# Encoder layer on one core: adaLN dots put at other places, one block sum dropped, loads and stores issued by three engines, and a fixed order in the gate stage

## The chip, the cores and the metric

The kernel runs on one core of a Trainium2 chip. The metric is the device time of one execution in microseconds; runs are compared by their median. The times before are 1262.81, 1264.8 and 1268.21 us.

Five engines run at once, each through its own instructions in its own order: TensorE (PE, matmuls), VectorE (DVE), ScalarE (ACT), GpSimd (POOL) and SyncE (SP). DMAs are issued by an engine, here by SP, POOL or ACT, and an issue waits in that engine's order until what it needs is free.

## The reference

One layer, 1024 positions, width 1024, all in float32:

```python
mod = jax.nn.silu(c) @ w_ada + b_ada
sh1, sc1, gt1, sh2, sc2, gt2 = jnp.split(mod[:, None, :], N_MOD, axis=-1)

h = rmsnorm(x, norm1_g) * (1.0 + sc1) + sh1
z = h @ w_in
...
a_out = gmlp_branch(u, v, gm_v_g, gm_w_s, gm_b_s) @ w_a
b_out = window_attention_branch(q, k, va, q_norm_g, k_norm_g, attn_sink) @ w_b
merged = jax.nn.sigmoid(gate_a) * a_out + jax.nn.sigmoid(gate_b) * b_out
x = x + gt1 * (merged @ w_o)

h2 = rmsnorm(x, norm2_g) * (1.0 + sc2) + sh2
f_gate, f_up = jnp.split(h2 @ w_ffn_in, 2, axis=-1)
x = x + gt2 * ((jax.nn.silu(f_gate) * f_up) @ w_ffn_out)
```

u, v, q, k, va and the two gates are column blocks of z. w_ada has 6 x 1024 columns; the kernel works in units of 128 of them (a *column* below), with 1024 numbers for each of 128 partitions.

## The kernel before, in words

**Products.** Every float32 product is made of three matmuls on a high and a low part of each operand (`mm3`). A weight unit of 128 x 1024 is loaded into a tile `raw` (three buffers, SP, L137), ACT copies its high part to `wh`, and DVE subtracts to get the low part `wl` (`unit`). PE waits for both.

**Stages**, in us of the profile: half 0 of the positions (q and k, v, attention, projections), 0 to 212; the q/k loop of half 1, 212 to 252; its v, u and attention, 252 to 350; its projection loop over d = 0 to 7, which here also prepares the gates (the *joint stage*), 358 to 404; the gates, 404 to 524; the output projection w_o, half 0 to 575 and half 1 to 627; then the FFN to the end.

**adaLN dots.** The first 16 columns are worked off at the start. 32 more stand in `ada_queue`, and the code takes them from it where it has a place: `ada_load` loads one column of 512 KB into a `raw` tile, `ada_next` lets DVE make the dot with silu(c) (one 128 x 1024 operation, and a small one for the result) and loads the next. `ada_half_load` loads a column as two halves into the two `hs` stream buffers, and `ada_half` makes two operations of 128 x 512 and two small ones. The places: six full dots in the d loop of half 0, five in the q/k loop of half 1 (k = 2, 3, 5, 6, 7), ten columns in the gate stage (five full, five in halves), eleven full ones in the output projection of half 0.

**Joint stage.** The gates of all d are computed by a scheme of Strassen's kind: seven products instead of eight (`GSTEP`, twelve matmuls each), on sums of blocks of the normalised x and on sums of blocks of the weights w_ga and w_gb. `block_sums(k, part, kinds)` makes the sums of x for a chunk k of four; it reads four chunk tiles a0, a1 (`hs`, two buffers) and b0, b1 (`xs`, two buffers), loaded from DRAM (x0d, x1sd) by `block_load`. Each sum has a high part (ACT) and a low part (DVE, `block_part`). The two parts of a chunk stand behind the projections d = 2k and 2k + 1. A projection's result for d > 1 is stored to `pd` (256 KB, POOL, L140).

**Gate stage.** For each d from 2 to 7 seven steps; step 6 of a d comes behind step 0 of the next. `gate_load(d + 1)` (two 512 KB loads of SP) comes behind step 3, `gate_prep_a`, `_b` and `_c` turn them into four weight units. `branch_load` brings 1 MB of `pd` back, `gating` combines it with the gates and stores to `md`; the output projection loads md through `m_load`.

**Order.** In each engine a scheduler places instructions by estimated readiness, except where `in_order[0]` is set: there they stay in the order of the code. Loads through `load` always stay in the code's order on SP. Rows of half 1 in the gate loop, the d loop and the o loop are those below.

## Time and profile before

| what | value |
|---|---|
| runs | 1262.81, 1264.8, 1268.21 us; median 1264.8 us |
| profiled execution, and its span | 1266.84 us, 1265.0 us |
| PE busy | 1227.7 us, 97% of the span, 5634 matmuls |
| DVE busy | 911.8 us, 72% |
| ACT busy | 574.0 us, 45% |
| POOL busy | 161.5 us, 13% |
| moved by DMA | 236.28 MB, mean 187 GB/s |

A busy PE can still be a slow one, since a matmul is counted as busy whatever clock was granted; that clock stands beside the busy times by stage. The chain of waits tells, for each stretch, what ended last. In rows of the time line, the bracket holds the engine's idle time ahead of a row and what ended it. Nearly all compute rows have line L76, that of the helper which records them; they are told apart by the names of their tiles.

### The profile page before, as it was taken

Reading aid. Unit: us, or ns where it says so; the run is one execution under the profiler, and the core shown is the slowest. Engines: PE = TensorE matmul, PEld = TensorE weight load, DVE = VectorE, ACT = ScalarE, POOL = GpSimd, SP = SyncE. Lnnn points to the kernel's source line nnn. Section 1 sums busy time; section 2 is a strip of 40 time slices with the busy share of each in tenths; the row PEclk is TensorE's granted clock in tenths of the full one; section 3 lists DMA queues with packets and bytes.
Section 4 is the critical chain, followed back from the end, with each engine's and each line's share of the span. In section 5 each row is a group of like instructions: output and inputs, shape, how many; then the busy total and the mean of one; then the engine's idle time right before and its main releaser. Section 6 shows DMA issues by size and latency. Waiting matters only on the chain.

```text
span 1265.0 us, 15583 instructions
## 1 busy us (share of the span) xinstructions
PE 1227.7 (97%) x5634; PEld 1012.8 (80%) x5634; DVE 911.8 (72%) x1496; ACT 574.0 (45%) x930; POOL 161.5 (13%) x202
## 2 busy tenths in 40 slices
PE   6999999899998999999999999999999999999998
PEld 4888887788886877767888888888888887888887
DVE  9898885387887787876798766677666676455646
ACT  5567854167866332434555233333332334433342
POOL 1223332023321000001100000000110000010001
PEclk9999999999999999999999999999999999999999
DMA  9632178422147445597721453554645549886652
GB/s 368 242 100 91 44 236 313 150 84 67 51 147 256 171 175 206 201 315 269 249 108 59 174 195 125 179 200 182 217 166 176 191 167 333 290 325 188 195 165 100
DMA packets 76272, 236.28 MB, mean 187 GB/s; under 512 B 9122, under 2 KB 9122, under 8 KB 70179
## 3 DMA queue, kind: packets, MB, share of 16 engines
q1 hardware_dynamic: 60626, 163.45, 38.2%
q0 software_dynamic: 15568, 71.84, 15.1%
q8 instruction: 44, 0.72, 0.2%
q14 instruction: 34, 0.27, 0.1%
HBM read 178.11 MB, written 57.15 MB: 186 GB/s over the span
## 4 chain that ended last, share of the span: by engine, by line
PE 63%; issue 12%; DMA 10%; DVE 9%; ACT 4%; POOL 0%; SPq 0%; ACTq 0%; DVEq 0%; POOLq 0%
PE mm L76 32%; PE at L76 31%; DVE mid L76 3%; DVE wl L76 2%; DMA raw<-in_w_gb_dram 2%; DMA raw<-in_w_o_dram 2%; DMA raw<-in_w_ada_dram 2%; ACT wh L76 1%; ACT mid L76 1%; DMA raw<-in_w_ab_dram 1%; DVE raw L76 1%; DMA mid<-in_w_ada_dram 1%; DMA wo<-in_w_out_dram 1%; ACT lb L76 1%; DMA wS<-wo 1%
## 5 line engine op out<-in xcount | busy, mean ns | idle before, releaser
L76 ACT CAST wh<-raw 128x1024 fp32r<-128x1024 f32 x155 | 162.6, 1052 | 183.9 <-PE mm L76 57.4
L76 DVE TENSOR_TENSOR wl<-raw,wh 128x1024 fp32r<-128x1024 f32 x141 | 172.2, 1222 | 96.3 <-ACT wh L76 92.4
L76 PE MATMUL mm<-mid,wh 128*128 128x512 f32 x704 | 218.9, 392 | 7.1 <-ACT wh L76 3.1
L76 PEld LDWEIGHTS mm<-mid,wh 128*128 128x128 f32 x704 | 131.7, 188 | 37.4 <-ACT wh L76 5.2
L76 PE MATMUL at<-j,wh 128*128 128x512 f32 x464 | 142.8, 389 | 0.0
L76 PE MATMUL mm<-mid,wl 128*128 128x512 f32 x352 | 138.5, 393 | 4.0 <-DVE wl L76 3.9
L76 PE MATMUL mm<-wh,h 128*128 128x512 f32 x384 | 129.9, 400 | 2.3 <-ACT h L76 2.1
L76 PEld LDWEIGHTS at<-j,wh 128*128 128x128 f32 x464 | 87.0, 188 | 18.2 <-ACT xs L76 0.2
L76 DVE TENSOR_TENSOR wl<-ws,wh 128x1024 fp32r<-128x1024 f32 (+1 forms) x55 | 62.0, 1128 | 43.7 <-ACT wh L76 43.7
L76 PE MATMUL mm<-j,wh 128*128 128x512 f32 x288 | 90.6, 396 | 0.0
L76 PE MATMUL at<-j,wl 128*128 128x512 f32 x232 | 90.3, 389 | 0.0
L76 PE MATMUL at<-h,wh 128*128 128x512 f32 x288 | 89.1, 391 | 0.7 <-DVE mid L76 0.7
L76 PEld LDWEIGHTS mm<-wh,h 128*128 128x128 f32 x384 | 72.0, 190 | 17.2 <-ACT h L76 3.0
L76 PE MATMUL mm<-h,wh 128*128 128x512 f32 x272 | 84.6, 392 | 0.0
L76 PEld LDWEIGHTS mm<-mid,wl 128*128 128x128 f32 x352 | 66.2, 188 | 21.8 <-DVE wl L76 8.3
L76 ACT CAST wh<-ws 128x1024 fp32r<-128x1024 f32 (+1 forms) x55 | 53.6, 974 | 59.0 <-DVE ws L76 42.5
L76 PE MATMUL mm<-wl,h 128*128 128x512 f32 x192 | 76.3, 397 | 0.1
L76 PEld LDWEIGHTS mm<-j,wh 128*128 128x128 f32 x288 | 55.1, 192 | 11.6
L76 PEld LDWEIGHTS at<-h,wh 128*128 128x128 f32 x288 | 53.8, 188 | 12.5 <-DVE mid L76 1.5
L76 DVE TENSOR_TENSOR ol<-raw,oh 128x1024 fp32r<-128x1024 f32 x30 | 36.7, 1224 | 31.7 <-ACT oh L76 31.5
L76 PEld LDWEIGHTS mm<-h,wh 128*128 128x128 f32 x272 | 50.6, 188 | 10.3
L76 ACT ACTIVATE xs<-xs 128x512 f32<-128x512 f32 x21 | 13.3, 633 | 97.2 <-DVE xs L76 97.2
(273 smaller groups left out, 2545.0 us busy)
## 6 DMA issues: line engine op xcount, KB each, us to landing
raw<-in_w_gate_dram SPq DMA_DIRECT2D x28, 512.0 KB, 5.1
raw<-in_w_ada_dram SPq DMA_DIRECT2D x27, 512.0 KB, 5.4
tA<-hid POOLq DMA_DIRECT2D x11, 1024.0 KB, 5.0
tB<-hid POOLq DMA_DIRECT2D x11, 1024.0 KB, 5.0
wo<-in_w_out_dram POOLq DMA_DIRECT2D x22, 512.0 KB, 6.3
wS<-wo POOLq DMA_DIRECT2D x11, 1024.0 KB, 5.2
raw<-wS SPq DMA_DIRECT2D x44, 256.0 KB, 3.8
raw<-tB SPq DMA_DIRECT2D x44, 256.0 KB, 4.3
```

The costliest lines, as they stand in the source:

```text
L76: ins = f(*args, **kw)
```

## The change: what it does

* **Dots.** The 32 columns are placed anew: five (not six) in the d loop of half 0; four in halves in the q/k loop of half 1, through `hs` and `xs` in turn, loaded at k = 2 and 3 and dotted at k = 4 to 7; five in halves in the attention steps 1 to 5 of half 1 (none before); twelve in halves in the gate stage (one in d = 2, three in d = 3, 4, 5 each, two in d = 6); four through `ada_pair_load`, two columns in one 1 MB load of POOL into a big buffer, in the output projection of half 0; two in halves at d = 0 and 1 of half 1.
* **One block sum less.** N2 is gone: step 3 uses T2 = b1 + a0, B22 is negated in place by ACT, and signs of the evictions change. A chunk has four sums and six low parts on DVE instead of five and six, in another order: b0 and a0 come free first.
* **Issuing engines.** Chunk loads, branch loads and md loads are issued by POOL instead of SP, the pd stores by ACT instead of POOL. SP keeps weights, x and halves of w_ada columns.
* **Gate stage.** It stays in the order of the code. `gate_load(d + 1)` comes right behind the steps 0 and 6 that open a d (in d = 2 behind step 1) instead of behind step 3. The projection of branch a for d = 7 is held back and runs behind step 1 of d = 2.
* The row statistics and modulations in the output projection of half 1 come somewhat later.

```diff
-    def ada_half_load():
+    def ada_half_load(tag="hs"):
...
+    def ada_pair_load():
+        i = ada_queue[0][0] - GT1
+        t = midt(F32, 2)
+        store(t, w_ada2[i : i + 2].rearrange("a p b -> p a b"))
...
-            load(chunk[name], (x0d if name[0] == "a" else x1sd)[4 * int(name[1]) + k])
+            store(chunk[name], (x0d if name[0] == "a" else x1sd)[4 * int(name[1]) + k])
...
             V.tensor_tensor(b1, b1, b0, op=ALU.subtract)
...
+            low3 = block_part("T3", k, b1, kinds[1], dsh[:, c])
+            V.tensor_tensor(b0, b0, a0, op=ALU.subtract)
+            low1 = block_part("T1", k, b0, kinds[1])
+            low3()
+            added(b1, a0)
+            low2 = t2()
...
+            block_load(k + 1, "b0")
+            for x in blk["B22"]:
+                A.activation(x[:, k, :], x[:, k, :].bitcast(F32), AF.Copy, scale=-1.0)
             return
...
+        low, low1 = b11(), b21()
+        low()
         low1()
-        block_load(k + 1, "b0")
+        block_load(k + 1, "a0")
+        V.tensor_tensor(a1, b1, a1, op=ALU.subtract)
+        low = block_part("T4", k, a1, kinds[2])
+        block_load(k + 1, "b1")
         low()
...
+        block_load(k + 1, "a1")
...
-    GSTEP = ((0, 0, "B11", 0), (1, 0, "T3", 1), (0, 1, "B21", 0), (2, 0, "N2", 2),
+    GSTEP = ((0, 0, "B11", 0), (1, 0, "T3", 1), (0, 1, "B21", 0), (2, 0, "T2", 2),
...
-        load(flat(branch_t[d]), pd[d])
+        store(flat(branch_t[d]), pd[d])
...
-            if hf == 1 and k == 1:
-                ada_load()
-            elif hf == 1 and k and k != 4:
-                ada_next(k < 7)
+            if hf == 1 and k in (2, 3):
+                ada_half_load(("hs", "xs")[k % 2])
+            elif hf == 1 and k > 3:
+                ada_half(("hs", "xs")[k % 2] if k < 6 else None)
...
+            if hf == 1 and 0 < s < 6:
+                ada_half("hs" if s < 5 else None)
...
-            for x in ("a1", "b0", "b1", "a0"):
+            for x in ("b0", "a0", "b1", "a1"):
...
+                if hf and d == KT - 1 and br == 0:
+                    held.append((wab[d], t))
+                    continue
...
-                    store(pd[d][:, j * Q : (j + 1) * Q], c)
+                    nc.scalar.dma_start(pd[d][:, j * Q : (j + 1) * Q], c)
...
-        load(t, md[hf][k])
+        store(t, md[hf][k])
...
+        if d == 2:
+            gate_step(d, 0)
+            gate_evict(d, 0)
+            gate_step(d, 1)
+            held_projection()
+            low_c = gate_prep_c(d)
+            gate_evict(d, 1)
+            low_c()
+            gate_load(d + 1)
...
         gate_step(d, 0)
         gate_evict(d, 0)
...
+        gate_step(d - 1, 6)
+        low_c = gate_prep_c(d)
+        gate_evict(d - 1, 6)
+        low_c()
+        if not last:
+            gate_load(d + 1)
...
-            gate_load(d + 1)
...
         if not last:
+            low_b()
+            if d in (3, 4, 5):
+                ada_half("hs")
+            low_s()
+            ada_half("hs" if d < KT - 2 else None)
...
-                ada_next()
-                if 2 < d < 6:
-                    ada_next()
+                if d in (0, 2):
+                    ada_pair_load()
+                if 0 < d < 5:
+                    ada_next(False)
+                if d == 7:
+                    ada_half_load()
```

What that does to the engines' orders is seen at three places. First DVE in the q/k loop of half 1. Before, a full dot (the rows with `silu_c`) stands between two low parts `wl` of the q and k weights:

```order
L76 TENSOR_TENSOR wl_2215<-raw_2212,wh_2214 128x1024
L76 SCALAR_TENSOR_TENSOR raw_2316,acc_mod<-raw_2316,silu_c 128x1024
L76 TENSOR_TENSOR wl_2258<-raw_2255,wh_2257 128x1024
L76 TENSOR_SCALAR mod<-acc_mod,cc 128x1
L76 SCALAR_TENSOR_TENSOR raw_2341,acc_mod<-raw_2341,silu_c 128x1024
L76 TENSOR_SCALAR mod<-acc_mod,cc 128x1
L76 TENSOR_TENSOR wl_2292<-raw_2289,wh_2291 128x1024
L76 SCALAR_TENSOR_TENSOR raw_2374,acc_mod<-raw_2374,silu_c 128x1024
L76 SCALAR_TENSOR_TENSOR mod<-acc_mod,badap,cc 128x1
```

After, the same stretch, from the low part that opens it; dots are halves from `hs` and `xs`:

```order
L76 TENSOR_TENSOR wl_2169<-raw_2128,wh_2168 128x1024
L76 SCALAR_TENSOR_TENSOR hs_2333,acc_mod<-hs_2333,silu_c 128x512
L76 TENSOR_TENSOR wl_2211<-raw_2208,wh_2210 128x1024
L76 SCALAR_TENSOR_TENSOR hs_2334,part_2395<-hs_2334,silu_c 128x512
L76 TENSOR_TENSOR acc_mod<-acc_mod,part_2395 128x1
L76 TENSOR_SCALAR mod<-acc_mod,cc 128x1
L76 TENSOR_TENSOR wl_2254<-raw_2251,wh_2253 128x1024
L76 SCALAR_TENSOR_TENSOR xs_2366,acc_mod<-xs_2366,silu_c 128x512
L76 TENSOR_TENSOR wl_2288<-raw_2285,wh_2287 128x1024
L76 SCALAR_TENSOR_TENSOR xs_2367,part_2431<-xs_2367,silu_c 128x512
```

The dots have moved some low parts further back, and none of them reads a `raw` tile any more.

Second, the loads of the joint stage. Before, SP issues chunk loads (`x0d`, `x1sd`) and the projection weights `w_ab` in one order:

```order
L137 DMA hs_3852<-x0d 128x512
L137 DMA raw_3858<-in_w_ab_dram 128x1024
L137 DMA hs_3903<-x0d 128x512
L137 DMA raw_3909<-in_w_ab_dram 128x1024
L137 DMA xs_3948<-x1sd 128x512
L137 DMA xs_3951<-x1sd 128x512
L137 DMA hs_3953<-x0d 128x512
L137 DMA raw_3959<-in_w_ab_dram 128x1024
L137 DMA hs_4004<-x0d 128x512
L137 DMA raw_4010<-in_w_ga_dram 128x1024
L137 DMA raw_4012<-in_w_gb_dram 128x1024
```

After, SP has the weights alone:

```order
L137 DMA raw_3860<-in_w_ab_dram 128x1024
L137 DMA raw_3915<-in_w_ab_dram 128x1024
L137 DMA raw_3966<-in_w_ab_dram 128x1024
L137 DMA raw_4017<-in_w_ab_dram 128x1024
L137 DMA raw_4068<-in_w_ga_dram 128x1024
L137 DMA raw_4070<-in_w_gb_dram 128x1024
L137 DMA hs_4204<-in_w_ada_dram 128x512
L137 DMA hs_4205<-in_w_ada_dram 128x512
```

and POOL has the chunk loads, with the stores to `md` of the first two d among them:

```order
L140 DMA hs_3900<-x0d 128x512
L140 DMA xs_3852<-x1sd 128x512
L140 DMA md_108<-t_778_3747 128x512
L140 DMA xs_3906<-x1sd 128x512
L140 DMA md_108<-t_780_3751 128x512
L140 DMA hs_3909<-x0d 128x512
L140 DMA hs_4004<-x0d 128x512
L140 DMA xs_3958<-x1sd 128x512
L140 DMA xs_4008<-x1sd 128x512
L140 DMA hs_4011<-x0d 128x512
L140 DMA hs_4108<-x0d 128x512
```

The chunk loads have left SP's order; in POOL's they stand one behind another and behind stores.

Third, DVE from the last steps of d = 3 in the gates to the first of d = 4. Before, a full dot from `raw` and one in halves stand among the evictions (`mid`) and the sums of weight blocks (rows of `raw` and `wl`):

```order
L76 TENSOR_TENSOR raw_4371<-raw_4371 128x512
L76 SCALAR_TENSOR_TENSOR raw_4416,acc_mod<-raw_4416,silu_c 128x1024
L76 SCALAR_TENSOR_TENSOR hs_4423,acc_mod<-hs_4423,silu_c 128x512
L76 TENSOR_TENSOR mid_4298<-at_4357,xs_4296 128x512
L76 TENSOR_TENSOR wl_4458<-raw_4371,wh_4457 128x1024
L76 SCALAR_TENSOR_TENSOR mid_4298<-mid_4298,mid_4213 128x2048
L76 TENSOR_TENSOR mid_4442<-mm_4467,xs_4440 128x512
L76 TENSOR_TENSOR mid_4298<-mid_4298 128x512 x2
L76 SCALAR_TENSOR_TENSOR mod<-acc_mod,badap,cc 128x1
L76 SCALAR_TENSOR_TENSOR hs_4424,part_4562<-hs_4424,silu_c 128x512
L76 TENSOR_TENSOR acc_mod<-acc_mod,part_4562 128x1
L76 SCALAR_TENSOR_TENSOR mod<-acc_mod,badap,cc 128x1
```

After, two columns in halves follow each other with three operations between, ahead of the next eviction and the low part of the last weight unit:

```order
L76 TENSOR_TENSOR wl_4464<-raw_4383,wh_4463 128x1024
L76 SCALAR_TENSOR_TENSOR hs_4424,acc_mod<-hs_4424,silu_c 128x512
L76 SCALAR_TENSOR_TENSOR hs_4425,part_4484<-hs_4425,silu_c 128x512
L76 TENSOR_TENSOR acc_mod<-acc_mod,part_4484 128x1
L76 TENSOR_SCALAR mod<-acc_mod,cc 128x1
L76 TENSOR_TENSOR raw_4381<-raw_4381,t_910_4460 128x512
L76 TENSOR_TENSOR raw_4381<-raw_4381 128x512
L76 TENSOR_TENSOR t_914_4467<-t_910_4460,t_913_4466 128x512
L76 SCALAR_TENSOR_TENSOR hs_4489,acc_mod<-hs_4489,silu_c 128x512
L76 SCALAR_TENSOR_TENSOR hs_4490,part_4496<-hs_4490,silu_c 128x512
L76 TENSOR_TENSOR acc_mod<-acc_mod,part_4496 128x1
L76 TENSOR_SCALAR mod<-acc_mod,cc 128x1
```

Both columns use the two `hs` buffers, so the load of the second stands behind the first one's operations.

More of the change, by code (lines that the diff above doesn't have):

```diff
@@ L531, in ada_half_load, with ada_half @@
             ada_halves.append((col, gain, t))
-    def ada_half(more=True):
+    def ada_pair_load():
+        i = ada_queue[0][0] - GT1
+        t = midt(F32, 2)
+        store(t, w_ada2[i : i + 2].rearrange("a p b -> p a b"))
+        for j in range(2):
+            col, gain = ada_queue.pop(0)
+            ada_ahead.append((col, gain, t[:, j, :]))
+    def ada_half(more=None):
         if not ada_halves:
@@ L544, in ada_half @@
         if more:
-            ada_half_load()
+            ada_half_load(more)
     def x_rows(hf, k):
@@ L1127, in half @@
                 else:
-                    gate_prep_b(2)
+                    gate_sums(2)
+                    for low in gate_prep_b(2):
+                        low()
             if hf and d == 5:
@@ L1165, with held_projection @@
     half(1)
+    def held_projection():
+        w, t = held.pop()
+        pb = at_bank()
+        for k in range(4):
+            kc = slice(k * P, (k + 1) * P)
+            mm3(pb, (w[0][:, kc], w[1][:, kc]), (t[0][:, k, :], t[1][:, k, :]), k == 0, k == 3)
+        c = tmp()
+        A.copy(c, pb)
+        nc.scalar.dma_start(pd[KT - 1][:, 2 * Q : 3 * Q], c)
     m0 = []
```

135 lines of the change are left out of this document (83 added, 52 removed).

## The prediction

> **What bounds the kernel now.** I read the page's totals first, then the busy time by stage, then the chain of waits in the stages that lose time, and last the rows of the engine that is waited for. The profiled execution took 1266.84 us, 1265.0 us of span and 1.84 around it. The sum below is made against 1266.84; the median of the three runs is 1264.8, so a change of so many us is taken off that median at the end. The totals:
>
> ```profile
> span 1265.0 us, 15583 instructions
> PE 1227.7 (97%) x5634; PEld 1012.8 (80%) x5634; DVE 911.8 (72%) x1496; ACT 574.0 (45%) x930; POOL 161.5 (13%) x202
> ```
>
> TensorE (PE) is the bound: 97%. The change removes no matmul, so all that can be won is time in which PE waits, or runs at a lower granted clock because it has waited. Busy time hides the second kind (a slow matmul counts as busy), so I count matmuls instead. The stages, in us from the span's start (length, busy time and instructions of each engine, granted clock, DMA share, GB/s):
>
> ```profile
> 212.00:252.00 40.00, 33.38 (x172) 28.10 (x171) 14.85 (x23) 6.67 (x8) 0.54 (x1) 0.96 0.50 163
> 282.00:324.00 42.00, 41.74 (x221) 35.48 (x220) 33.76 (x96) 29.33 (x73) 12.24 (x7) 1.00 0.16 51
> 360.00:404.00 44.00, 43.28 (x191) 35.37 (x191) 35.16 (x50) 23.54 (x35) 6.56 (x12) 1.00 0.61 210
> 404.00:416.00 12.00, 8.27 (x23) 6.00 (x22) 11.58 (x18) 7.23 (x11) 1.08 (x2) 0.72 0.59 221
> 416.00:508.00 92.00, 89.88 (x391) 72.63 (x390) 70.22 (x113) 29.85 (x41) 4.34 (x8) 1.00 0.52 191
> 508.00:575.00 67.00, 62.09 (x263) 48.27 (x263) 55.89 (x87) 25.91 (x39) 4.34 (x8) 1.00 0.77 262
> 575.00:627.00 52.00, 52.00 (x239) 43.28 (x238) 37.27 (x49) 22.86 (x29) 6.51 (x11) 1.00 0.77 270
> 627.00:1265.00 638.00, 632.39 (x2789) 521.21 (x2787) 417.88 (x536) 239.38 (x302) 40.07 (x72) 1.00 0.54 186
> ```
>
> The yardstick for a 128x512 matmul at full clock is this piece of the chain, twelve of them in 2.72 us, or 0.2267 each:
>
> ```profile
> 1016.85 2.72 PE mm L76 x12
> ```
>
> By it 404 to 416 holds 23 x 0.2267 = 5.2 us of matmuls in 12 (6.8 lost), 416 to 508 holds 391 x 0.2267 = 88.6 in 92 (3.4 lost), and 508 to 575 holds 263 x 0.2267 = 59.6 in 67 (7.4 lost). The half-1 q/k loop, 212 to 252, has shorter matmuls; there the chain gives the loss. The last stage (the FFN, 638 us) keeps its order, so I cost it at nothing. Everything that can be won is in about 27 us.
>
> **Part 1, the q/k loop of half 1.** The chain there:
>
> ```profile
> 206.82 6.95 DMA raw<-in_w_ada_dram
> 215.13 4.43 DMA raw<-in_w_ada_dram
> 222.59 3.97 DMA raw<-in_w_ada_dram
> 229.31 6.03 DMA raw<-in_w_ada_dram
> 244.44 1.83 PE mm L76 x8
> 248.26 1.83 PE mm L76 x8
> ```
>
> Two equal places of successive k-steps lie 248.26 - 244.44 = 3.82 us apart, so eight steps need 30.6 us. The stage has 40.0, so 9.4 are lost. The four waits are DVE's: an adaLN dot waits for its 512 KB of w_ada, and behind it in DVE's order stand the low parts (wl) of the next projection weights, for which PE waits. After the change the rows of w_ada come through the stream buffers, asked for two k-steps (7.6 us) ahead, and the dots stand at k = 4 to 7. The waits of the first steps are gone. Late next are two lows that stand behind a dot: one column costs DVE
>
> ```profile
> 415.81 0.68 DVE L76 SCALAR_TENSOR_TENSOR hs<-hs,silu_c 128x512 f32<-128x512 f32 x1
> 417.34 0.22 DVE L76 SCALAR_TENSOR_TENSOR mod<-acc_mod,badap,cc 128x1 f32<-128x1 f32 x1
> ```
>
> 417.56 - 415.81 = 1.75 us. If the rows are there, the two lows are late by part of a column, 1.2 us in all: -8. If rows land after the 9.3 us that such loads have taken (row below), each of three dots ahead of a low is 9.3 - 7.6 = 1.7 late, 5.1 in all: -4. I take -6.5, with 2.9 lost: the loads share the queue with the weights, as in that 9.3, but fewer stand ahead.
>
> **Part 2, attention of half 1** gets five dot columns, 5 x 1.75 = 8.75 us of DVE. Its place in each step (five in the 42 us of the window, 8.4 each) is ahead of the normalising, where DVE idles now:
>
> ```profile
> 289.38 0.16 DVE L76 TENSOR_TENSOR den<-den,es 128x4 f32<-128x4 f32 x1 [1.52 <-ACT es L76]
> 292.11 0.62 DVE L76 CUSTOM_DVE_ANT_0 lb<-at,bias,nsink 128x384 f32<-128x384 f32 x1 [0.32 <-PE at L76]
> ```
>
> 1.52 + 0.32 = 1.84 us idle against 1.75: hidden, barely. Without that cover it costs up to 8.75. I take +0.5, bounds 0 and +3 (a third uncovered).
>
> **Part 3, the joint stage.** One chunk of block sums stands on DVE for every two projections of PE, 24 matmuls each, 48 x 0.2267 = 10.9 us. The same sum of three successive chunks:
>
> ```profile
> 376.30 0.69 DVE L76 TENSOR_TENSOR xs<-xs,xs 128x512 f32<-128x512 f32 x1 [0.51 <-DMA xs<-x1sd]
> 390.05 0.69 DVE L76 TENSOR_TENSOR xs<-xs,xs 128x512 f32<-128x512 f32 x1
> 404.42 0.68 DVE L76 TENSOR_TENSOR xs<-xs,xs 128x512 f32<-128x512 f32 x1
> ```
>
> 13.75 and 14.37 us apart: slower than PE, which therefore has nothing to do at the end:
>
> ```profile
> 406.86 0.49 PE L76 MATMUL mm<-mid,wh 128*128 128x512 f32 x1 [2.27 <-ACT mid L76]
> 408.82 0.80 PE L76 MATMUL mm<-mid,wh 128*128 128x512 f32 x1 [1.46 <-DVE mid L76]
> 409.84 1.05 PE L76 MATMUL mm<-j,wh 128*128 128x512 f32 x2
> 411.12 1.05 PE L76 MATMUL mm<-j,wh 128*128 128x512 f32 x2
> ```
>
> Behind two waits of 2.27 and 1.46, three matmuls take 411.12 - 409.84 = 1.28 us, 0.427 each, against 0.68: this slow stretch is about 3 of the 6.8 lost. (A slow stretch therefore costs about 3 us besides the wait that brings it.) A chunk's sums wait for chunk loads, and SP issues these in its order:
>
> ```profile
> 394.85 0.32 SPq L137 DMA_DIRECT2D hs<-x0d  x1
> 395.22 0.43 SPq L137 DMA_DIRECT2D raw<-in_w_ga_dram  x1
> ```
>
> The chunk load stands ahead of the gate weights, which go out 0.37 us behind it, however long it waited for its buffer. Landing times (median us from issue, last number):
>
> ```profile
> hs<-x0d SPq DMA_DIRECT2D x8, 256.0 KB, 3.1
> xs<-x1sd SPq DMA_DIRECT2D x8, 256.0 KB, 4.7
> pd<-t POOLq DMA_DIRECT2D x24, 256.0 KB, 5.6
> out_dram<-mid POOLq DMA_DIRECT2D x12, 256.0 KB, 2.5
> hs<-in_w_ada_dram SPq DMA_DIRECT2D x10, 256.0 KB, 9.3
> ```
>
> After the change a chunk is ten DVE operations of 0.69 and a low of 1.22, 8.1 us, and a reload of b1 of which about 1.9 (the operations behind its last reader) are covered. With landing L the cycle is 8.1 + L - 1.9: 10.2 at 4.0, under PE's 10.9; 11.8 at 5.6, over it. The first chunk began near 376.30 - 13.75 = 362.5, so the last one will begin at 362.5 + 3 x 10.9 = 395.3 with L = 3.7 (PE sets the pace; 396 with what DVE does between), and at 362.5 + 3 x 11.8 = 398 with 5.6, which I put at 400.5 for POOL's queue (issues and stores ahead of each load), against 404.42. Behind these sums, 8.5 us later, stands the second low of the gate weights, for which gate step 1 waits. PE is there after 15 projections and step 0, 16 x 2.72 = 43.5 us from 358, at 401.5. So it waits 404.5 - 401.5 = 3 us, where 7.5 are lost now (6.8 above, and 0.7 of the 44 us before): a gain of 4.5. Or it waits 409 - 401.5 = 7.5 and runs slowly for a loss of 3 besides: 3 worse than now. Between, 7.5 / 1.9 = 3.9 us per us of landing. No row shows a load of POOL in this stage. I take L = 4.0, near the mean of the first two rows (3.9): -4.5 + 0.3 x 3.9 = -3.3, bounds -6 (half the wait gone) and +3. The projection that is held back runs behind step 1, so it cannot cover that wait. POOL's own queue gains up to 16 chunk loads, and its md stores wait for DVE ahead of some; ACT gets the 12 pd stores of a half, of this kind:
>
> ```profile
> 373.97 0.54 POOL L140 DMA_DIRECT2D pd<-t  x1 [1.06 <-ACT t L76]
> ```
>
> ACT is busy for 23.54 of 44 us here; at 0 to 0.54 each (POOL's price; no row shows ACT's) 6.5 us more at most are hidden.
>
> The Trainium skill, "SBUF — State Buffer", section "SBUF: two separate sides", speaks against the move: while DVE runs some two-port operations, POOL cannot write the descriptors of its DMAs, which then start late. The 5.6 against 3.1 us in the rows above would agree, the 2.5 of out_dram would not; by the rule the 5.6 case holds.
>
> **Part 4, the gate stage** loses 3.4 us now. One piece:
>
> ```profile
> 504.82 0.73 PE L76 MATMUL mm<-mid,wh 128*128 128x512 f32 x2 [0.94 <-ACT wh L76]
> ```
>
> The weights of the next d are loaded behind step 3 and come late; after the change behind step 0, three steps (8.2 us) earlier. Against that DVE's work grows. A cycle is 7 x 2.72 = 19.04 us; DVE is busy for 70.22 of 92, so idle for 4.5 of a cycle. The third dot takes 1.75, and a full dot made in halves 0.4 more: 2.3 stay at best, 0 at worst if the idle time now is all waiting in order. I take half, 1.15. The second dot of a pair needs a reload of the same buffers: the load goes out when the first half's dot is over, and the second half (0.66), two small operations (0.44) and three of 0.6 stand between, 2.9 us. The nearest row for a short queue, the 3.1 of x0d, leaves 0.2 to wait: within the slack. I take -2 (bounds -3 and +4: the 4.7 row would leave 1.8 of wait, 0.65 over the slack, in each of three cycles, and one slow stretch of about 2).
>
> **Part 5, half 0 of the output projection** loses 7.4, because dots and w_o share the three raw buffers:
>
> ```profile
> 541.48 8.00 DMA raw<-in_w_o_dram
> 551.92 5.20 DMA raw<-in_w_o_dram
> 559.52 3.95 DMA raw<-in_w_o_dram
> ```
>
> 17.15 us of the chain are waits for w_o. Afterwards the 11 loads of 512 KB for dots are gone from raw; four dots come in two 1 MB loads elsewhere. DVE is rid of 7 columns, DMA of some 3 MB of 67 x 0.262 = 17.6. What stays late is m0's rows, loaded by POOL at the end of the gates: about 1.4. I take -6, bounds -7 (all but 0.4) and -1.5 (the late start of w_o stays).
>
> **Part 6, half 1 of it** gets two dots and bunched modulations: 239 matmuls fill the 52 us, DVE is busy for 37.27, so +0.5 (0 to +2).
>
> **The sum:** -6.5 + 0.5 - 3.3 - 2 - 6 + 0.5 = -16.8, so 1266.84 - 16.8 = 1250.0 for a profiled run, and 1264.8 - 16.8 = **1248.0** for the median. All best ends together give -24.0 (1241), all worst ones +6.5 (1271).
>
> **Rivals.** *The issuing engine buys nothing* (the move doesn't do what it is made for): the loads wait for buffers, whoever issues them. Then part 3 and part 4 give 0: 1248 + 3.3 + 2 = 1253.3. For it: a chunk load at 394.85 needs its buffer free first, from any engine. Against it: the next in line, w_ga at 395.22, went out as soon as SP was past it. The Trainium skill, "DMA: Bandwidth & Descriptors", section "Issuing engines are not separate DMA queues", says the same: only the sequencer's issue time is saved.
>
> *POOL's loads land at 5.6*: part 3 is +3, and m0's rows are 2 us later (the 1.6 by which 5.6 passes 4.0, and a little of queue): 1248 + 6.3 + 2 = 1256.3. For it: the row of pd, stored by POOL in this very stage. Against it: 2.5 for out_dram.
>
> *Attention has no room*: the five columns cost 8.75 instead of 0.5: 1248 + 8.25, again 1256.3. For it: 1.84 against 1.75. Against it: PE there has 41.74 of 42 and ACT only 29.33, so DVE is not the bound yet.
>
> *The pair's reload stalls the gates* (slower): if it takes the 9.3 of the row, DVE waits 9.3 - 2.9 = 6.4 in d = 3, 4 and 5, behind it the low of the third gate weight and an eviction, and PE behind those. Less 1.15 of slack, 5.25 x 3 = 15.8, three slow stretches of 3 are 9, and the 2 of part 4 are lost: 1248 + 26.8 = 1275. It costs from a landing of about 4 us, and passes the old time near 6: 3 x (6 - 4.05) + 9 + 2 is the 16.8 won. Against it: the loads of that row are issued right behind a branch, both gate weights and a full column; after the change the weights have landed long before.
>
> **Chances.** Forecast 0.57, first rival 0.11, second 0.13, third 0.08, the slower one 0.11. A measurement of this kernel tells about 0.5% (6.3 us) from no change: faster is below 1258.5. A third of the second and third rivals' chance, and a little of the forecast's, may end within it: faster 0.76, same 0.13, slower 0.11. The range goes from 1239 (just past the best ends) to 1265, which leaves out the slower rival and the worst ends together.
>
> **What would show it.** Right: no wait of 4 us for w_ada in the q/k loop; sums of chunks about 11 us apart, and under 4 us of PE waits around step 1; no wait for w_ga or w_gb; no chain through w_o. Wrong: DVE waiting for hs in the middle of a gate cycle, chunk cycles of 12 us or more with DMA as releaser, a granted clock below 1 in the gates, or attention steps longer than 8.4 us.

## The result, and the profile after

The changed kernel takes 1272.38 us (median of 14 runs, 1268.23 to 1281.33) against 1265.18 us before (14 runs, 1260.0 to 1271.93). The ratio is 1.0068, with a 95% interval of 1.0045 to 1.0090: it is slower by 0.7%, where a gain of 16.8 us was forecast. The page of the changed kernel begins:

```profile
span 1272.2 us, 15652 instructions
PE 1232.7 (97%) x5634; PEld 1016.3 (80%) x5634; DVE 915.1 (72%) x1545; ACT 577.7 (45%) x938; POOL 170.5 (13%) x216
```

The span is 7.2 us longer with the same 5634 matmuls. To see where, I cut both traces at the same matmuls, counted in order of time, so that a stage holds the same number of them in each. The busy times of the changed kernel in these stages (columns as in the prediction; the last row is a closer look at the start of the FFN):

```profile
212.45:248.43 35.98, 33.42 (x171) 28.00 (x170) 14.37 (x31) 6.72 (x9) 0.00 (x0) 0.95 0.50 163
278.25:326.39 48.14, 44.59 (x221) 36.61 (x219) 41.24 (x125) 29.47 (x73) 12.33 (x7) 0.96 0.32 110
360.18:427.23 67.05, 59.25 (x243) 46.35 (x242) 46.72 (x65) 38.19 (x60) 11.90 (x18) 0.95 0.66 213
427.23:527.19 99.96, 99.96 (x442) 82.77 (x441) 90.70 (x158) 36.09 (x50) 9.20 (x17) 1.00 0.56 191
527.19:571.20 44.01, 43.99 (x192) 35.61 (x191) 32.72 (x49) 18.48 (x28) 10.72 (x19) 1.00 0.78 262
571.20:627.23 56.03, 53.02 (x238) 42.88 (x237) 37.06 (x55) 21.41 (x28) 6.94 (x10) 1.00 0.75 264
627.23:646.95 19.72, 16.67 (x66) 13.43 (x65) 13.46 (x19) 9.40 (x14) 1.58 (x2) 0.83 0.42 155
631.00:637.00 6.00, 4.74 (x17) 3.86 (x18) 3.95 (x6) 5.41 (x7) 1.04 (x1) 0.72 0.29 85
```

The gates and half 0 of the output projection now run without a gap: PE is busy for 99.96 of 99.96 and 43.99 of 44.01 us. But attention, the joint stage, half 1 of the projection and the start of the FFN each lose more than these gain. Here is each stage's length in us, beside what was forecast for it, and in every kernel that was tried ("o1" is half 1 of the output projection with the first 66 matmuls of the FFN):

| kernel | q/k loop | attention | joint | gates | o0 | o1 |
|---|---|---|---|---|---|---|
| before | 39.9 | 42.0 | 62.8 | 103.7 | 51.0 | 65.0 |
| changed | 36.0 | 48.1 | 67.1 | 100.0 | 44.0 | 75.8 |
| difference | -3.9 | +6.1 | +4.3 | -3.7 | -7.0 | +10.8 |
| forecast | -6.5 | +0.5 | -3.3 | -2 | -6 | +0.5 |
| e_att_small | 33.1 | **44.4** | 67.1 | 100.0 | 44.3 | 75.4 |
| e_joint_sp | 31.6 | 46.8 | **66.7** | 100.0 | 45.0 | 73.2 |
| e_o1_map | 32.8 | 46.9 | 66.5 | 100.4 | 44.3 | **72.1** |
| e_o1_nodots | 37.1 | 48.6 | 67.9 | 100.8 | **45.7** | **67.7** |
| e_att_pool | 35.2 | **42.6** | 67.2 | 100.0 | 45.7 | 76.9 |
| e_joint_order | 32.0 | 46.8 | **62.4** | 100.0 | 44.0 | 74.5 |
| e_back | 35.6 | **42.1** | 64.8 | 100.5 | **48.4** | **65.0** |
| e_back_order | 34.8 | **42.1** | **63.5** | 100.0 | **48.8** | **65.0** |
| e_o1_pool | 33.4 | 46.4 | 66.9 | 100.0 | 43.9 | **69.5** |
| e_best | 33.5 | **42.6** | **63.2** | 100.0 | **44.4** | **71.4** |
| e_best7 | 32.5 | **42.6** | **63.3** | 100.0 | **44.0** | **66.7** |
| e_best_b1 | 33.5 | **42.6** | **62.7** | 100.0 | **44.1** | **66.4** |

Bold stages are those which an edit touches; each length is that of one execution. The others show how much a stage moves by itself: attention 46.4 to 48.6, o1 73.2 to 76.9, the joint stage 66.5 to 67.9 and once 64.8 (e_back), the q/k loop, which no edit touches, 31.6 to 37.1. A kernel's one time therefore says less here than the length of the stage.

### The profile page after: what moved, and what is told of

Same layout as the page of the kernel before. It is cut to its first block, busy times and chain, and to the rows that moved or that the text cites. A ratio compares the mean times of both kernels' runs of the same rounds, so it can differ in the third digit from the quotient of the medians.

```text
span 1272.2 us, 15652 instructions
## 1 busy us (share of the span) xinstructions
PE 1232.7 (97%) x5634; PEld 1016.3 (80%) x5634; DVE 915.1 (72%) x1545; ACT 577.7 (45%) x938; POOL 170.5 (13%) x216
## 4 chain that ended last, share of the span: by engine, by line
PE 52%; issue 16%; DVE 12%; DMA 12%; ACT 6%; POOL 1%; SPq 0%; ACTq 0%; POOLq 0%; DVEq 0%
PE at L76 29%; PE mm L76 23%; DVE mid L76 3%; DVE wl L76 2%; ACT wh L76 2%; DMA wo<-in_w_out_dram 1%; DMA raw<-in_w_o_dram 1%; DMA xs<-x1sd 1%; DVE lb L76 1%; DVE xs L76 1%; ACT lb L76 1%; DMA hs<-in_w_ada_dram 1%; DMA wS<-wo 1%; DMA xs<-in_xT_dram 1%; DMA mid<-in_w_ada_dram 1%
## 5 line engine op out<-in xcount | busy, mean ns | idle before, releaser
L76 PE MATMUL mm<-mid,wh 128*128 128x512 f32 x696 | 215.5, 390 | 1.6 <-ACT wh L76 1.2
L76 PE MATMUL mm<-mid,wl 128*128 128x512 f32 x348 | 135.5, 390 | 0.8 <-DVE wl L76 0.6
L76 DVE TENSOR_TENSOR wl<-ws,wh 128x1024 fp32r<-128x1024 f32 (+1 forms) x55 | 62.0, 1128 | 44.4 <-ACT wh L76 44.4
L76 ACT CAST wh<-ws 128x1024 fp32r<-128x1024 f32 (+1 forms) x55 | 53.6, 974 | 58.8 <-DVE ws L76 42.1
L76 PE MATMUL mm<-j,wl 128*128 128x512 f32 x144 | 57.5, 399 | 0.9 <-DVE wl L76 0.9
```

The costliest lines, as they stand in the source:

```text
L76: ins = f(*args, **kw)
```

## The experiments

**Attention: the dots, or the loads that feed them?** The forecast had walked DVE only. What SP does there, before:

```profile
266.58 6.29 SPq L137 DMA_DIRECT2D raw<-in_w_u_dram  x2
275.09 0.33 SPq L137 DMA_DIRECT2D raw<-in_w_gb_dram  x1
```

and after (a row with a count spans from its first issue to the end of its last, waits included):

```profile
263.23 22.39 SPq L137 DMA_DIRECT2D hs<-in_w_ada_dram  x4
285.72 0.38 SPq L137 DMA_DIRECT2D raw<-in_w_u_dram  x1
294.72 0.94 SPq L137 DMA_DIRECT2D hs<-in_w_ada_dram  x2
295.76 0.38 SPq L137 DMA_DIRECT2D raw<-in_w_gb_dram  x1
```

The second column's load stands ahead of the weights w_u and w_gb, and waits for the `hs` buffers which the first dot has to free. The weights go out only at 285.72 and 295.76, 7.5 and 17.5 us into the stage; before the change they had left some 9 and 7 us ahead of it. ACT's cast of them stands ahead of its casts of the probabilities:

```profile
290.44 1.05 ACT L76 CAST wh<-raw 128x1024 fp32r<-128x1024 f32 x1 [1.75 <-DMA raw<-in_w_u_dram]
```

and DVE waits for those:

```profile
292.13 1.89 DVE L76 TENSOR_TENSOR pL<-at,pH 128x512 fp32r<-128x512 f32 x3 [1.63 <-ACT pH L76]
```

The first experiment takes DVE's work away and leaves the loads:

```diff
-                ada_half("hs" if s < 5 else None)
+                ada_half("hs" if s < 5 else None, 16)
```

> The changed kernel with one edit: the five adaLN columns in the attention of half 1 are still loaded whole, but only 16 of each 512 numbers are multiplied (the rest of these dots is left out of the computation). The attention steps took 42.0 us before and 48.1 after the change. Theory A1, the dot operations stand on DVE in the softmax's chain: the stage falls back to 42 to 43 us, the total falls by about 5. Rival A2, the loads of the halves hold the weights behind them up in SP's order, and ScalarE's cast of those weights stands ahead of the casts of the probabilities: the loads are as before, so the stage stays at 46.5 to 48.

Attention took 44.4 us: between the two. Shorter dots also free the buffers sooner (w_gb left 15.6 us into the stage, not 17.5), so this run doesn't separate the causes. The next one leaves the dots whole and takes only their loads off SP:

```diff
-                load(t[i], w_ada2[col - GT1][:, i * 512 : (i + 1) * 512])
+                (issue or load)(t[i], w_ada2[col - GT1][:, i * 512 : (i + 1) * 512])
...
-                ada_half("hs" if s < 5 else None)
+                ada_half("hs" if s < 5 else None, store)
...
```

> The changed kernel with one edit: the half columns of the attention steps are loaded by POOL instead of SP; the dots stay whole. The attention steps took 42.0 us before, 46.8 to 48.6 with the change in four kernels that do not touch them, 44.3 with the dots cut to 16 numbers. In the cut kernel the loads of w_u still left SP 9 us later than before the change, because the second column's load waits there for its buffer. Theory A2 (SP's order holds the weights up): 44 to 45 us, the weights leave SP 8 us ahead of their use again. Theory A1 alone (the dots' 1.75 us on DVE): no change, 46.8 or more. Both in part: between, near 46. POOL makes some low parts in this stage, so a wait of its own queue could give some of it back.

42.6 us. SP has the weights out early again:

```profile
254.75 13.57 SPq L137 DMA_DIRECT2D raw<-in_w_u_dram  x3
270.53 0.33 SPq L137 DMA_DIRECT2D raw<-in_w_gb_dram  x1
```

So the loss was SP's order (A2), and five whole dots on DVE cost 0.6 us once their loads are out of it. Behind SP's order the dots' length did count: 3.7 us went when they were cut. (The total, 1270.7 us in a single run, didn't show this: attention gave back 5.5 of its 6.1 us, while o1 was 1.1 and half 0 of the projection 1.6 longer than in the changed kernel.)

**Joint stage: POOL's loads, the reload, or the order on DVE?** In the changed kernel PE waits 4.78 us for gate step 1:

```profile
412.03 1.22 PE L76 MATMUL mm<-j,wh 128*128 128x512 f32 x2 [4.78 <-ACT wh L76]
```

Ahead of it on DVE stands the last chunk, and the sums of the weight blocks that ACT has to cast (at 409.01 and 410.21) come among its sums:

```profile
405.08 0.69 DVE L76 TENSOR_TENSOR xs<-xs,xs 128x512 f32<-128x512 f32 x1 [0.98 <-DMA xs<-x1sd]
...
409.01 0.68 DVE L76 TENSOR_TENSOR t<-raw 128x512 f32<-128x512 f32 x1
409.61 0.68 DVE L76 TENSOR_TENSOR hs<-xs,hs 128x512 f32<-128x512 f32 x1
410.21 0.68 DVE L76 TENSOR_TENSOR raw<-raw,raw 128x512 f32<-128x512 f32 x1
```

Before the change they stood ahead of the last chunk's sum at 404.42:

```profile
403.08 0.69 DVE L76 TENSOR_TENSOR t<-raw 128x512 f32<-128x512 f32 x1 [0.43 <-DMA raw<-in_w_gb_dram]
403.81 0.69 DVE L76 TENSOR_TENSOR raw<-raw,raw 128x512 f32<-128x512 f32 x1
```

DVE also waits for the reload of b1, as the reload of the third chunk shows, issued at 387.84 and there at 394.48, 6.6 us later:

```profile
387.84 0.54 POOL L140 DMA_DIRECT2D xs<-x1sd  x1 [1.63 <-DVE hs L76]
```

```profile
394.48 0.69 DVE L76 TENSOR_TENSOR xs<-xs,xs 128x512 f32<-128x512 f32 x1 [5.44 <-DMA xs<-x1sd]
```

First, chunk loads by SP again:

```diff
-            store(chunk[name], (x0d if name[0] == "a" else x1sd)[4 * int(name[1]) + k])
+            load(chunk[name], (x0d if name[0] == "a" else x1sd)[4 * int(name[1]) + k])
```

> The changed kernel with one edit: the 16 chunk loads of the block sums are issued by SP again, instead of by POOL. From the start of the joint stage to the end of the fourth gate product it took 62.8 us before and 67.0 after the change, and DVE waited 2.9, 5.4 and 1.0 us for reloaded chunk tiles. Theory B1, POOL's issue makes these loads land late: they land in 3 to 4 us instead of 3.7 to 6.5, and the stretch falls to about 62 us. Rival B2, the reload is asked for too late whoever issues it, because the new order frees the first tile of the next chunk last: the waits stay within 1 us of those, and the stretch stays at 66 to 68, or grows when the loads stand behind weights.

66.7 us against 67.1: the stage is as long with either engine, and B1's 62 us did not come. The rows of b0 and b1 (`xs`) landed sooner, those of a0 and a1 (`hs`) later. The changed kernel's rows for POOL's issues:

```profile
hs<-x0d POOLq DMA_DIRECT2D x8, 256.0 KB, 3.6
xs<-x1sd POOLq DMA_DIRECT2D x8, 256.0 KB, 3.8
```

and those of this kernel for SP's:

```profile
xs<-x1sd SPq DMA_DIRECT2D x8, 256.0 KB, 2.7
hs<-x0d SPq DMA_DIRECT2D x8, 256.0 KB, 6.1
```

A reload of b1 issued by SP at 377.63 took 7.4 us, but it was asked for earlier in the stage, and DVE waited only 1.47 us for it:

```profile
385.08 0.69 DVE L76 TENSOR_TENSOR xs<-xs,xs 128x512 f32<-128x512 f32 x1 [1.47 <-DMA xs<-x1sd]
```

So B2 was right on the length, but not on the waits: this one and the second chunk's sums (17.0 us into the stage, not 20.7) came about 4 us earlier than with POOL's loads. The last chunk began no earlier, with its tile in time: 44.6 us into the stage (399.68 - 355.06) against 44.9 (405.08 - 360.18). And PE's wait at step 1 got longer, not shorter:

```profile
407.54 1.22 PE L76 MATMUL mm<-j,wh 128*128 128x512 f32 x2 [6.99 <-ACT wh L76]
```

Here it is ACT's order: ahead of the cast stands the eviction of a projection, which waits until an earlier pd store has landed and freed its tile:

```profile
405.95 0.59 ACT L76 COPY t<-mm 128x512 f32<-128x512 f32 x1 [3.19 <-DMA pd<-t]
406.43 1.05 ACT L76 CAST wh<-raw 128x1024 fp32r<-128x1024 f32 x1
```

Both kernels point at what stands ahead of this weight unit on DVE and ACT (B3). The next one keeps the order of the code from d = 6 on, where the weight sums stand between the two parts of the last chunk:

```diff
-            in_order[0] = d < 2
+            in_order[0] = d < 2 or (hf == 1 and d > 5)
...
-            in_order[0] = False
+            in_order[0] = hf == 1 and d > 5
```

> The changed kernel with one edit: in the joint stage of half 1 the projections and sums from d = 6 on stay in the order of the code, as the gate stage does, so that the sums of the weight blocks and the low part for gate step 1 stand ahead of the second part of the last chunk's sums on DVE. Joint stage and the first gate steps (to the mark at 420.46 of before) took 62.8 us before, 66.6 to 67.9 in four kernels with the change, whoever issued the chunk loads. Theory B3, what PE waits for at step 1 is the place of these weight sums behind ten operations of the last chunk: 61 to 63.5 us, the wait of 5 us there falls under 2. Rival B2, the late reload of the chunk tiles sets the end: 66 us or more, since the same reloads come first in either order.

62.4 us, 4.6 less than with the change. PE's wait at step 1 is gone, and one of 2.61 us stands 9 us ahead of it, where the changed kernel had 1.19:

```profile
396.89 1.22 PE L76 MATMUL mm<-mid,wh 128*128 128x512 f32 x2 [2.61 <-ACT wh L76]
...
405.72 0.61 PE L76 MATMUL mm<-j,wh 128*128 128x512 f32 x2
```

DVE in this kernel:

```profile
399.44 0.68 DVE L76 TENSOR_TENSOR xs<-xs,xs 128x512 f32<-128x512 f32 x1
...
402.94 0.68 DVE L76 TENSOR_TENSOR t<-raw 128x512 f32<-128x512 f32 x1
403.66 0.69 DVE L76 TENSOR_TENSOR raw<-raw,raw 128x512 f32<-128x512 f32 x1
```

B3's range held, for DVE and ACT together, since the edit keeps both in order. But the weight sums moved little: 4.2 us behind the chunk's first sum, not 5.1. Step 1 begins 50.3 us into the stage (405.72 - 355.44) instead of 51.9 (412.03 - 360.18), which is 1.6 of the 4.6 us. The other 3.0 lie behind it: in the changed kernel matmuls come 0.43 us apart from 412 to 418 there, behind the wait of 4.78 us, and here 0.23 apart. What the late reload costs besides (B2: DVE still waits 4.47 us for a b1) is not settled by this run; e_best_b1 below tries it.

**Half 1 of the projection: late statistics, dots, or their loads?** Two places wait in the changed kernel. PE waits for the row statistics:

```profile
597.53 0.71 PE L76 MATMUL at<-ident,rcol 128*128 128x128 f32 x4 [2.39 <-POOL rcol L76]
```

and for the last modulation at the start of the FFN, after which matmuls come 0.43 us apart for a while:

```profile
631.98 0.50 PE L76 MATMUL at<-h,wh 128*128 128x512 f32 x1 [2.77 <-ACT h L76]
...
635.54 0.63 PE L76 MATMUL at<-h,wl 128*128 128x512 f32 x1
635.97 0.63 PE L76 MATMUL at<-h,wh 128*128 128x512 f32 x1
```

The clock granted there is 0.72 to 0.83 (last two rows of the stages above). Statistics and modulations put back where they were, the dots left:

```diff
-                if hf == 1 and (d, k) == (2, 0):
-                    col_rstd(sums[0], NT, rcol[2])
-                if hf == 1 and (d, k) == (3, 3):
-                    rb = spread(rcol[2], NT)
...
-                for i in {3: (0, 1), 4: (2,), 5: (3, 4), 6: (5,), 7: (6,)}.get(d, ()):
+                if d == 1:
+                    col_rstd(sums[0], NT, rcol[2])
+                elif d == 2:
+                    rb = spread(rcol[2], NT)
+                for i in {2: (0,), 3: (1, 2), 4: (3,), 5: (4,), 6: (5,), 7: (6,)}.get(d, ()):
```

> The changed kernel with one edit: in half 1 of the output projection the row statistics, their spread and the modulations stand where they stood before the change (behind d = 1, 2, and one or two a step from d = 2); the two dot columns at d = 0 and 1 stay. From the start of this half to 13 us into the FFN it took 65.0 us before and 75.8 after. Theory C1, the later statistics push the modulations against the end: 66 to 68 us. Rival C2, the two dot columns and their loads delay DVE and the input rows at d = 0 and 1, and all that follows: 73 us or more.

72.1 us: the FFN starts without a loss, but PE's wait for the statistics has grown from 2.39 to 4.13 us, and 7 us stay. The other way round, the dots moved away and the late statistics left:

```diff
-                if d < 2:
-                    ada_half(None if d else "hs")
...
-                if d in (0, 2):
+                if d in (0, 2, 4):
...
```

> The changed kernel with one edit: the two dot columns of half 1 of the output projection move to half 0 as a third pair load (six columns there); statistics and modulations stay late. Stretch from the start of half 1 to 13 us into the FFN: 65.0 us before, 75.8 after. Theory C1 (late statistics and bunched modulations): it stays at 73 us or more. Rival C2 (the dot columns): it falls to 66 to 69 us. Half 0 of the projection, 44.0 us now against 51.0 before, grows by 0 to 2 us for two more columns.

67.7 us: the dots are the greater part (8 of 10.8); the late statistics may be the rest. The whole kernel took 1274.62 us in its one run; the FFN behind these matmuls, where nothing was edited, was 4.3 us longer than in the changed kernel. Why two dots of 1.75 us cost 7 is seen on DVE and SP of the changed kernel. A dot waits for its rows, and the eviction (`t<-mm,mod,xs`) stands behind it:

```profile
582.90 0.69 DVE L76 SCALAR_TENSOR_TENSOR hs<-hs,silu_c 128x512 f32<-128x512 f32 x1 [2.23 <-DMA hs<-in_w_ada_dram]
...
584.13 0.75 DVE L76 SCALAR_TENSOR_TENSOR t<-mm,mod,xs 128x512 f32<-128x512 f32 x1
```

Only the eviction frees the x tile that SP's next load needs, and the weights w_o stand behind that load:

```profile
584.90 0.33 SPq L137 DMA_DIRECT2D xs<-in_xT_dram  x1
585.32 0.38 SPq L137 DMA_DIRECT2D raw<-in_w_o_dram  x1
```

So the same two loads by POOL, with the statistics in their old place:

```diff
-                    ada_half(None if d else "hs")
+                    ada_half(None if d else "hs", store)
...
-                    ada_half_load()
+                    ada_half_load("hs", store)
```

> The changed kernel with two edits: in half 1 of the output projection the statistics, spread and modulations stand as before the change, and the two dot columns that stay there are loaded by POOL instead of SP. From the start of this half to 13 us into the FFN: 65.0 us before, 75.8 after the change, 72.0 with the same statistics and SP's loads, 65.0 without the dots. Theory C3, SP's order (a dot waits for its rows, the eviction behind it on DVE holds the x tile that SP's next load needs, and w_o stands behind that load): 65.5 to 68 us. Rival C2 in its plain form (two dot columns, 3.5 us, on DVE at a bad place): 70 to 72.

69.5 us, between the two ranges. Half 1 alone, 52.0 before, took 53.6, against 59.0 with SP's loads: C3 explains 5.4 of the 7. (In five kernels that leave this half alone it moved by 3 us, 55.0 to 58.0.) The other 2.9 us fell at the start of the FFN, in a slow stretch behind waits of only 0.52 and 0.28 us.

**Put together.** First the dots taken back out of both stages:

```diff
-            if hf == 1 and 0 < s < 6:
-                ada_half("hs" if s < 5 else None)
...
-                if 0 < d < 5:
-                    ada_next(False)
+                if 0 < d < 6:
+                    ada_next(False)
+                    ada_next(False)
...
```

> The changed kernel with its placements of dots in the two stages that lost taken back: none in the attention of half 1 and none in half 1 of the output projection, whose statistics and modulations stand as before the change; ten columns come through five pair loads in half 0 of it, and six instead of five in the d loop of half 0. If the losses of these stages belong to the dots there (A1, A2, C2 and C1 together), attention takes 42 to 43 us, half 1 with the start of the FFN 65 to 67, against 48.1 and 75.8; half 0 of the projection grows from 44 to 45 to 48 for six more columns. Total 1255 to 1259. If the new places cost as much, 1263 or more.

Attention 42.1 and o1 65.0, as before the change; six more columns in o0 cost 4.4 us there, a little over the upper end, and 1259.92 us in its one run is over it too. With the order of the joint stage besides (the diff of the joint stage above):

> The kernel with the dots taken back out of attention and out of half 1 of the output projection, and with the order of the code kept in the joint stage from d = 6 on. If B3 holds besides, it is 4 us below the one without that order: 1251 to 1255, ratio to before 0.989 to 0.992. If B2 holds, it is the same as that one.

1257.37 us (10 runs), a ratio of 0.9951, interval 0.9932 to 0.9971. It is faster than before, but by less than expected, and the joint stage was 1.3 us shorter than in e_back, not 4. In e_back, with the changed kernel's order, PE still waits 4.76 us at step 1, but step 1 begins 50.2 us into the stage and not 51.9; why is open. With the order of the code it began at 51.1, no sooner, and what was won again lies behind it: from step 1 to the end of the stage 12.4 us against 14.5. Then the dots kept in attention, with POOL's loads, and six columns in o0 (the diffs above together):

> The changed kernel with the losses taken out: attention's five columns loaded by POOL, none in half 1 of the output projection, six in half 0, its statistics as before the change, and the order of the code in the joint stage from d = 6 on. Stage by stage against before, from the runs so far: q/k loop -4 to -8, attention +0.6, joint stage with its first gate steps -0.4 to +0.7, gates -3.7, half 0 of the projection -5.3, half 1 and start of the FFN 0. Sum -12 to -17 if these add up; total 1248 to 1253, ratio 0.987 to 0.991. If the columns only move their cost about, it is no better than the 0.995 of the kernel that took the dots out of attention.

1254.56 us (6 runs, 1252.44 to 1258.26) against 1265.13, a ratio of 0.9913, interval 0.9894 to 0.9932. This is 1.6 us above the expected range, but the version beats both kernels. It was meant to have nothing left in o1, and its profile, that of the slowest of the six runs, still shows 71.4 us there: the last modulations are late again, here behind a row of x1 that landed late,

```profile
610.55 0.75 DVE L76 SCALAR_TENSOR_TENSOR mid<-hs,mod,at 128x512 f32<-128x512 f32 x1 [0.83 <-DMA hs<-x1d]
```

and a slow stretch follows PE's wait of 1.73 us:

```profile
616.42 0.50 PE L76 MATMUL at<-h,wh 128*128 128x512 f32 x1 [1.73 <-ACT h L76]
```

e_best_b1 below, with the same code in this half, took 66.4, so some of this belongs to the one execution. Two variants of it. Seven columns in attention, four in o0:

```diff
-            if hf == 1 and 0 < s < 6:
-                ada_half("hs" if s < 5 else None)
+            if hf == 1 and 0 < s:
+                ada_half("hs" if s < 7 else None, store)
...
```

> As the kernel with the losses taken out, but with seven columns in the attention (all steps from 1 to 7, loaded by POOL) and four, not six, in half 0 of the projection. If DVE has 1.84 us a step free there as the profile of before shows, attention costs another 0 to 1 us and half 0 gains 1.5: 1247 to 1252. If DVE's room is used up at the last steps, attention grows by 2 us or more, and it is no faster than the other.

Attention stays at 42.6, the stretch behind it grows by 1.5 (34.0 to 35.5 us), o0 gains 0.4, not 1.5: 1254.7 us in its one run, above the range and no better. And the sum that frees b1 put earlier, for chunks 0 to 2:

```diff
-        V.tensor_tensor(a1, b1, a1, op=ALU.subtract)
-        low = block_part("T4", k, a1, kinds[2])
-        block_load(k + 1, "b1")
-        low()
...
+        V.tensor_tensor(a1, b1, a1, op=ALU.subtract)
+        low1 = block_part("T4", k, a1, kinds[2])
+        block_load(k + 1, "b1")
+        low = b11()
```

> As the kernel with the losses taken out, with one edit in the block sums of chunks 0 to 2: the sum that frees the tile which the next chunk needs first (a1 = b1 - a1) stands at the head of the second part, and the low part of B21, which it waits for, in the first part. Theory B2 as what is left of the joint stage's loss (DVE waits of 3.1 and 4.5 to 5.5 us for this reload): the waits shrink by about 1.5 us each and the stretch falls by 1 to 3 us; total 1 to 3 us below. If the reload's landing is set by traffic instead, it moves by under 1 us.

The joint stage went from 63.2 to 62.7 us, and the total, 1255.7 us (4 runs, ratio 0.9929, interval 0.9904 to 0.9954), is the same within its interval. Yet DVE's waits for the reload did shrink, and by more than expected: from 3.11 and 5.25 us to 1.02 and 2.77, with one of 2.16 new at the last chunk. Step 1 began 48.7 us into the stage instead of 50.8. What was won there was lost behind it, since PE was at step 1 sooner too and waited longer. e_best, and then e_best_b1:

```profile
403.27 0.73 PE L76 MATMUL mm<-j,wh 128*128 128x512 f32 x2 [0.71 <-ACT wh L76]
```

```profile
400.56 0.74 PE L76 MATMUL mm<-j,wh 128*128 128x512 f32 x2 [3.21 <-ACT wh L76]
```

Behind the longer wait the matmuls ran slowly for a while, and the rest of the stage took 13.9 us against 12.4. So the late reload does delay DVE (B2), but it no longer sets the length of this stage by itself.

## Why the prediction was wrong, step by step

* **Part 1, q/k loop: right way, the size too large, and the step only half right.** -3.9 us for -6.5. "The waits of the first steps are gone" is not so: DVE still waits 6.92, 6.36 and 1.95 us for w_ada. The rows were not there ahead of their dots: SP issued those of the second column at 216.02, behind a weight at 215.60, when DVE, done with the work ahead, was already waiting.

```profile
221.93 0.69 DVE L76 SCALAR_TENSOR_TENSOR xs<-xs,silu_c 128x512 f32<-128x512 f32 x1 [6.36 <-DMA xs<-in_w_ada_dram]
```

```profile
223.82 0.58 PE L76 MATMUL mm<-wl,h 128*128 128x512 f32 x1 [2.00 <-DVE wl L76]
```

What fell is PE's wait for the low part behind such a dot: 0.37, 0.19 and 2.00 us where it was 1.55 and 4.95, which is the whole gain. The thirteen kernels with the same code there lie between 31.6 and 37.1 us, -6.0 in the mean, so the size of -6.5 is near what the code does.
* **Part 2, attention: failed.** +6.1 for +0.5, outside the bound of +3. "Hidden, barely" was right for what it counted: with the loads off SP's order the five dots cost 0.6 us (e_att_pool), against +0.5. What it left out is the other half of the step that was moved: ten loads in SP's order, ahead of the weights, one of which waits for a buffer that a dot frees. That cost 5.5 us. The third rival had the stage and a like size (8.25), but the wrong cause: DVE had the room.
* **Part 3, joint stage: failed.** +4.3 for -3.3. The step that failed is the cycle of 10.9 us, which let the last chunk begin at 395 to 396, 38 us into the stage. It began 44.9 us into it. The three cycles (columns as in the prediction):

```profile
362.63:380.83 18.20, 18.20 (x82) 15.08 (x81) 15.29 (x22) 11.92 (x20) 4.08 (x7) 1.00 0.70 213
380.83:394.48 13.65, 13.65 (x62) 11.31 (x61) 8.14 (x12) 6.44 (x10) 2.15 (x4) 1.00 0.76 262
394.48:405.08 10.60, 8.74 (x37) 6.26 (x36) 8.98 (x12) 7.72 (x12) 2.41 (x5) 1.00 0.50 157
```

DVE's 8.1 us for a chunk were right for the second, but in the first it is busy for 15.3, with the gating of d = 0 and 1 and three weights' low parts among the sums. And the landing was mis-sized where it counts: the median of these loads is 3.8 (4.0 were taken), but the reloads of b1, for which DVE waited, took 5.4, 6.6 and 3.8. The next step held: the second low of the gate weights ended 8.8 us behind the first of these sums, for 8.5. So step 1 came 51.9 us into the stage, not at 46.5 to 47. PE was there at 47.1, waited 4.78 us and ran slowly behind that; the whole stage lost 12.0 us (67.1 less 243 x 0.2267) where it had lost 7.7. The order of the code from d = 6 on shortens that wait to between 0 and 3.2 us: 62.4 to 63.5 us in the five kernels with it, 64.8 to 67.9 in the eight without. The second rival (loads of POOL at 5.6) had the reload's landing nearly right, but not its cause, since one of SP's took 7.4; the first was right in that the engine which issues changes nothing in the stage's length (e_joint_sp). The Trainium skill, "SBUF — State Buffer", section "SBUF: two separate sides", which spoke for late starts of POOL's DMAs under some of DVE's operations, gets no support from the medians in this stage, 3.6 and 3.8 us by POOL and 2.7 and 6.1 by SP; whether DVE's operations here are of that kind, no run shows.
* **Part 4, gates: right.** -3.7 for -2, a little past the better bound of -3; all that was lost there came back, and the reload of the second dot of a pair stalls PE nowhere (DVE waits for such rows once, 0.58 us). The rival on the slower side, placed here, did not happen.
* **Part 5, half 0 of the projection: right.** -7.0 for -6: PE is idle for only 0.02 us there, and the 1.4 us set aside for m0's late rows did not come.
* **Part 6, half 1: failed worst.** +10.8 for +0.5. The step was one line: PE fills the stage and DVE is busy for 37.27 of 52. Neither says when the last operation of a chain is done. Two dots made a loop of DVE's order and SP's order, worth 5.4 us by e_o1_map against e_o1_pool; the late statistics and the slow stretch at the start of the FFN are the rest. How much of the loss at the FFN's start belongs to which is open: it was 0 to 0.1 us in three kernels, 5.7 in e_best without any dot in this half, 0.8 in e_best_b1 with the same code here as e_best, and 6.7 with the change.

The sum of the measured terms is -3.9 + 6.1 + 4.3 - 3.7 - 7.0 + 10.8 = +6.6 of the span's 7.2; the forecast for the same six was -16.8. The two stages in which dots were added at little price by DVE's count make 16 us of that difference. All worst ends together gave 1271; the kernel is past even that, because three of the six bounds were too narrow. The chance of 0.11 for a slower kernel stood on the gates alone, so its direction came true by luck. The Trainium skill, "DMA: Bandwidth & Descriptors", section "Issuing engines are not separate DMA queues", says that another issuing engine saves only the sequencer's time to issue, usually small. For the chunk loads the stage's length agrees (66.7 and 67.1 us). For attention it doesn't: moving ten loads from SP to POOL took 4 to 6 us off, since an issue that waited there for its buffer held up the weights behind it.

## What to carry to other kernels

When work is moved to an idle place on one engine, walk every queue that its loads enter: a load that waits for a buffer stops the weights behind it, and the engine that would free the buffer may itself be waiting for those. Put a load whose buffer is freed late on a queue in which nothing urgent stands behind it. A stage that PE fills to 100% has no room at its end just because DVE is idle for a quarter of it: the last chain of small operations decides.

## What the runs showed of the hardware

* Waits of 1.73 and 0.28 us in e_best were followed by slow matmuls: the first 66 of the FFN took 18.7 us against 13.0 before, 3.7 more than these waits, at a granted clock of 0.82. Waits of 1.39 and 0.28 us at the same place in e_joint_sp were not (15.2 us, clock 1.00), but 0.52 and 0.28 us in e_o1_pool were (15.9 us, clock 0.89). The length of the wait alone doesn't decide it.
* Behind a wait of 3.2 to 7.0 us for gate step 1 the rest of the joint stage took 13.9 to 15.2 us in nine kernels (16.5 in a tenth, with one more wait of 2.94 us); behind waits of at most 0.7 us it took 12.2 to 12.4 in three.
* A DMA issue costs ACT and SP 0.33 us and POOL 0.54 (medians of the changed kernel). Results stored to pd landed after 5.6 us (median) when POOL issued them, and when ACT did after 4.8 in the changed kernel and 5.5 in e_joint_sp.
* The q/k loop took 31.6 to 37.1 us in thirteen kernels with the same code there.
